# Stick-breaking scores from stacked key parts: two passes over doubled queries in place of three over a block diagonal

## The chip, the cores and the metric

The kernel runs on one core of one Trainium2 chip. The metric is the device time of one execution in microseconds: 546.92 us, the median of three runs (546.83 to 547.07). The engines are called PE (TensorE), DVE (VectorE), ACT (ScalarE), POOL (GpSimd) and SP (SyncE). PEld is PE's loading of the stationary operand, which overlaps the matmuls.

## The reference, cut to what matters

One layer of a decoder over 256 tokens of width 1024: a half-step feed-forward network, a mixer with two attentions side by side, a second half-step network, a final norm. All is float32. The change is in the second attention, stick-breaking, with 8 heads of 64:

```python
def stick_breaking_attention(q, k, v):
    z = einsum('bhqd,bhsd->bhqs', q, k) * scale          # scores, scale = 64 ** -0.5
    past = s_pos[None, :] < t[:, None]
    log_fail = where(past, log_sigmoid(-z), 0.0)
    later = cumsum(log_fail, axis=3, reverse=True) - log_fail
    w = where(past, exp(log_sigmoid(z) + later), 0.0)
    return einsum('bhqs,bhsd->bhqd', w, v)
```

A key's weight is its own sigmoid times the product of the failures of all keys between it and the query. A key later than the query has no weight, so of the 256 x 256 scores of a head the block of late keys (128 to 255) and early queries (0 to 127) isn't computed.

## The kernel before, in words

**Precision.** Each float32 operand is split into a high part in the matmul's format (fp32r) and the low rest, also fp32r. A product is three passes: high x high, high x low, low x high. `split` (L400) makes the two parts: a cast on ACT (L401), then a subtraction on DVE (L402). The weights stream in as tiles of 128 x 512 and are split the same way (L232 and L233 with a gain, L228 and L229 without), up to `AHEAD` = 7 tiles ahead of the matmul that uses them, in `WB` = 12 buffers.

**PE's order** is written out by hand. `unit` (L374) issues the three matmuls of 512 columns of one weight tile and one block of 128 tokens, then calls `weave.tick()` and `W.pump()`. So a tick, or step, is one unit of PE's stream. `Weave` (L102) holds generators that do the rest of the work: each runs to its next `yield d` and is due again d steps later. Those marked `long` (the two attention lanes) move one at a time per step, and after the others. `flush(long=True)` runs all of them to their ends without waiting for their steps.

**What sets the order of the others.** PE and SP follow the program's order. In this part of the kernel the instructions of ACT, DVE and POOL are put in order at compile time by a planner, from priorities and its own costs; on the chip each of these engines then takes its work strictly in that order.

**The mixer.** `project` (L876) makes one of ten projections of 512 columns: 8 weight tiles x 2 blocks of tokens = 16 units. In order: q, k, v of the MoBA attention (`heads(0, "a", ...)`), q, k, v of the stick-breaking one (`heads(3, "b", ...)`), four for the gates. Two lanes (L1080) run the attentions by pairs of heads between the units: pairs 0 and 2 in lane 0, pairs 1 and 3 in lane 1, MoBA first (`moba_pair`: scores S at L1006, then the softmax, the transposes `ptp` at L1024, the values `y_a` at L989), then stick-breaking (`stick_pair`). After the gates come the branch products `ba` and `bb`. After the first eight units of `ba` the lanes are flushed (L1141).

**q and k of the stick-breaking heads, turned.** A projection has tokens on the partitions; the scores need the head's 64 values there. DVE transposes 32 x 32 squares (L917) into `qsb` and `ksb`, and an exchange of 16 DMAs of 32 KB (`exchange`, L526), eight from SP and eight from POOL, moves the squares to their partitions in `qmb` and `kmb`. One step issues one DMA on each of the two queues. `D_LANDED` = 6 steps later the pieces are split, `D_PIECE` = 2 steps between them. k becomes `kThb` and `kTlb` (two casts of 128 x 512, two subtractions). q becomes a block diagonal, `bdhb` and `bdlb`, in two tiles each: with two heads on the 128 partitions, the columns of one head hold its queries on its 64 rows and zeros on the other 64 (eight memsets on POOL at L958, four casts and four subtractions of 64 x 512). `D_READY - D_PIECE` = 5 steps after the last piece, q or k is marked there, and `stick_pair` may start.

**The scores** (L1044 to L1047): one matmul with the block diagonal gives both heads, with 128 rows of contraction of which half meet zeros. `pass3` (L974) issues the three passes: 512 columns for the first 128 keys (2 heads x 256 queries), 256 columns for the last 128 keys (2 heads x 128 queries). Six matmuls and 2304 columns a pair, four pairs.

**Then**, at steps 7, 6, 6 and 6 apart (`D_STICK`): three activations on ACT, `sp` and its split on DVE with a mask on POOL between; the sums over later keys as matmuls with a triangle (L1064 to L1066); the exponential (L1068), mask and split to `wwh` and `wwl`; the product with the values (`values`, L989, `y_b`).

The tiles of 1024 columns named here (`big`, L281) share 20 buffers.

Of the kernel before, what the change touches and what calls it, by code (L numbers as in the profile page):

```python
# [8 lines left out]
F32 = mybir.dt.float32  # L9
# [8 lines left out]
P = 128  # L18
# [6 lines left out]
HD = 64  # L25
# [19 lines left out]
D_MOVE = 2  # L45
D_MOVED = 12
D_LANDED = 6
D_PIECE = 2
D_ROTATED = 14, 10
D_READY = 7  # L50
# [210 lines left out]
def hybrid_layer_kernel(ctx, tc, x, xt, pos, g_final, bgate, wstream, out):  # L261
    nc = tc.nc
# [18 lines left out]
    def big(nm, dt=F32R):  # L281
        return work.tile([P, 1024], dt, name=nm, tag="big", bufs=20)
# [12 lines left out]
    first = consts.tile([P, 3 * KD + T], F32, name="first")  # L295
# [45 lines left out]
    ident = consts.tile([P, P], F32, name="ident")  # L341
# [58 lines left out]
    def split(dst_h, dst_l, src, hi_engine=None, rest=nc.vector):  # L400
        (hi_engine or nc.scalar.copy)(dst_h, src)  # L401
        rest.tensor_sub(dst_l, src, dst_h.bitcast(F32))  # L402
# [105 lines left out]
    def lagged(n, lag):  # L508

        for k in range(n + lag):  # L510
            if k < n:
                yield 0, k
            if k >= lag:
                yield 1, k - lag

    def slots(q, n):

        return q[:, 0:n * P].rearrange("p (g s w) -> p s g w", g=4, s=n)

    def plain(q):
        return q.rearrange("p (s g w) -> p s g w", g=4, w=32)

    def exchange(moved, squares, n, queues, gap):  # L526

        w = 32
        for m in range(16):
            i, j = divmod(m, 4)  # L530
            queues[m % len(queues)].dma_start(moved[j * w:j * w + w, i * n * w:(i + 1) * n * w],  # L531
                                              squares[i * w:i * w + w, j * n * w:(j + 1) * n * w])
            if m % len(queues) == len(queues) - 1:
                yield gap
# [361 lines left out]
        g.tensor_mul(t2[:, :, 8:16], d3[:, :, 0:8], sin[:, t, 8:16].unsqueeze(1).to_broadcast([P, NH, 8]))  # L896
        marks["rot"] = g.tensor_add(d3[:, :, 0:16], t1, t2).ins

    def heads(b0, nm, res, rotary, diagonal):


        for j, which in enumerate("qk"):
            src = {}
            squares = None if rotary else big(f"{which}s{nm}", F32)

            def evac(t, ps, j=j, which=which, src=src, squares=squares):
                dst = row512(f"{which}{nm}{t}")
                if j == 0:
                    if nm == "a":
                        nc.gpsimd.tensor_scalar(rq[t], un[t].r, 0.125, None, op0=ALU.mult)  # L910
                    nc.scalar.activation(dst, ps, AF.Copy, scale=rq[t])
                else:
                    nc.scalar.activation(dst, ps, AF.Copy, scale=un[t].r)
                if rotary:
                    rotate(dst, t)
                else:
                    nc.vector.transpose(slots(squares, 8)[:, t:t + 7:2], plain(dst))  # L917
                src[t] = dst

            def turn(which=which, src=src, squares=squares):  # L920
                if rotary:
                    tp = two_banks(f"{which}tp{nm}")
                else:
                    tp = big(f"{which}m{nm}", F32)
                    yield from exchange(tp, squares, 8, [nc.sync, nc.gpsimd], 1)
                    yield D_LANDED
                for pr in range(4 if rotary else 0):
                    for t in range(2):
                        nc.tensor.transpose(tp[:, pr * 256 + t * P:pr * 256 + (t + 1) * P], src[t][:, pr * P:(pr + 1) * P], ident)
                if which != diagonal:  # L930
                    parts = big(f"{which}Th{nm}"), big(f"{which}Tl{nm}")
                    for c in range(2):
                        s = slice(c * 512, c * 512 + 512)
                        if rotary:
                            split(parts[0][:, s], parts[1][:, s], tp[:, s])
                        else:
                            split(plain(parts[0][:, s]), plain(parts[1][:, s]), slots(tp, 8)[:, c * 4:c * 4 + 4])
                            yield D_PIECE
                    ready = [[q[:, pr * 256:(pr + 1) * 256] for q in parts] for pr in range(4)]
                else:  # L940
                    tp4 = slots(tp, 8).rearrange("p (c t) g w -> p c t g w", t=2)
                    for c in range(2):
                        for j in range(2):
                            rows = slice(j * HD, j * HD + HD)
                            dst = [q[rows].rearrange("p (c j t g w) -> p c j t g w", c=2, j=2, t=2, g=4)[:, :, j] for q in res["bd"][c]]
                            split(dst[0], dst[1], tp4[rows, c * 2:c * 2 + 2])
                            yield D_PIECE
                    ready = [[q[:, pr % 2 * 512:pr % 2 * 512 + 512] for q in res["bd"][pr // 2]] for pr in range(4)]
                yield D_READY if rotary else D_READY - D_PIECE
                res[which] = ready  # L950

            if which == diagonal:
                res["bd"] = [(big(f"bdh{nm}{c}"), big(f"bdl{nm}{c}")) for c in range(2)]
                for c in range(2):
                    for q in res["bd"][c]:
                        for half in range(2):
                            q5 = q[half * HD:(half + 1) * HD].rearrange("p (c j t) -> p c j t", c=2, j=2)
                            nc.gpsimd.memset(q5[:, :, 1 - half, :].bitcast(F32), 0.0)  # L958
            project(b0 + j, evac)
            weave.add(turn(), D_ROTATED[j] if rotary else D_TURNED)  # L960

        vs = big(f"vh{nm}"), big(f"vl{nm}")

        def evac_v(t, ps):
            s = slice(t * 512, t * 512 + 512)
            nc.scalar.activation(vs[0][:, s], ps, AF.Copy, scale=un[t].r)
            nc.vector.scalar_tensor_tensor(vs[1][:, s], ps, un[t].r, vs[0][:, s].bitcast(F32),
                                           op0=ALU.mult, op1=ALU.subtract)
            if t == 1:
                res["v"] = [[q[:, s * 512:(s + 1) * 512] for q in vs] for s in range(2)]  # L970

        project(b0 + 2, evac_v)

    def pass3(o, a, b, first, last):  # L974
        for i, (p, q) in enumerate(((0, 0), (0, 1), (1, 0))):
            nc.tensor.matmul(o, a[p], b[q], start=first and i == 0, stop=last and i == 2, skip_group_check=True)

    def two(ap, w):
        return ap.rearrange("p (j w) -> p j w", w=w)
# [59 lines left out]
    def stick_pair(pr, b, y):  # L1039
        while "q" not in b or "k" not in b:  # L1040
            yield 0
        q, k = b["q"][pr], b["k"][pr]

        z = two_banks(f"z{pr}")  # L1044
        z0, z1 = two(z[:, 0:512], 256), two(z[:, 512:768], 128)
        pass3(z[:, 0:512], [e[:, 0:128] for e in k], q, True, False)
        pass3(z1, [e[:, 128:256] for e in k], [two(e, 256)[:, :, 128:256] for e in q], True, False)  # L1047
        zz = z[:, 0:768]
        e = wide(f"e{pr}")

        nc.scalar.activation(e, zz, AF.Abs)
        nc.scalar.activation(e, e, AF.Exp, scale=-1.0)
        nc.scalar.activation(e, e, AF.Ln, bias=1.0)
        b["z", pr] = True
        yield D_STICK[0]
        sp = wide(f"sp{pr}")
        nc.vector.scalar_tensor_tensor(sp, zz, 0.0, e, op0=ALU.max, op1=ALU.add)
        earlier(sp)
        sh, sl = wide_r(f"sh{pr}"), wide_r(f"sl{pr}")
        split(sh, sl, sp, nc.vector.tensor_copy)  # L1060
        yield D_STICK[1]
        for i, s in enumerate((sh, sl)):
            s1 = two(s[:, 512:768], 128)
            nc.tensor.matmul(z[:, 0:512], tri, s[:, 0:512], start=False, stop=False, skip_group_check=True)  # L1064
            nc.tensor.matmul(z1, tri, s1, start=False, stop=i == 1, skip_group_check=True)
            nc.tensor.matmul(z0[:, :, 128:256], ones, s1, start=False, stop=i == 1, skip_group_check=True)  # L1066
        w = wide(f"w{pr}")
        marks["exp"] = nc.scalar.activation(w, zz, AF.Exp).ins  # L1068
        earlier(w)
        yield D_STICK[2]  # L1070
        wh, wl = wide_r(f"wwh{pr}"), wide_r(f"wwl{pr}")
        split(wh, wl, w, nc.vector.tensor_copy)
        yield D_STICK[3]
        while "v" not in b:
            yield 0
        values(pr, b["v"], [two(e[:, 0:512], 256) for e in (wh, wl)], [two(e[:, 512:768], 128) for e in (wh, wl)], y, "b")

    a, b, ys = {}, {}, {}
# [22 lines left out]
    weave.add(lane(0), 36, long=True)  # L1101
    weave.add(lane(1), 42, long=True)
    heads(0, "a", a, True, None)
    heads(3, "b", b, False, "q")


    gates = {}
# [23 lines left out]
    for c in range(2):  # L1131
        banks = {}
        for t, k in lagged(4, 2):
            if k == 0:
                banks[t] = acc_bank(f"ba{t}{c}")
            i = W_BR + c * 4 + k
# [153 lines left out]
```

## Time and profile before

| | |
|---|---|
| median of three runs | 546.92 us (546.83 to 547.07) |
| profiled execution | 547.5 us |
| its span, first to last instruction | 545.8 us |
| PE busy | 538.0 us, 99% of the span, 2460 matmuls |
| weight loads (PEld) busy | 444.4 us, 2460 loads |
| DVE busy | 453.5 us, 83% |
| ACT busy | 355.5 us, 65% |
| POOL busy | 122.1 us, 22% |
| mean granted PE clock | 0.997 |

Times are microseconds; the duration of a single instruction in a group is in ns. A matmul's length in the trace holds the latency of the pipeline, so that neighbours overlap; what one costs is the distance from its start to the next one's. A group row gives line, engine, operation, output <- inputs, shapes, count, then busy time, mean ns of one, and the engine's idle time just before, with what ended it. A row for a tile has the least, median and greatest duration, and the first and last start. The chain of waits is the chain of work that ended last, with start and length of each piece.

### The profile page before, as it was taken

The page shows a single profiled execution, that of the slowest core. Times are in us where ns is not written, and L with a number is a line of the kernel's source. Part 1 is how long each engine was busy: PE and PEld are TensorE (multiplying, and loading weights), DVE is VectorE, ACT ScalarE, POOL GpSimd, SP SyncE. Part 2 cuts the span into 40 slices and gives each one's busy share as a digit, 9 for nine tenths or more (in the row PEclk, how much of TensorE's full clock was granted, in tenths as well). Part 3 has the DMA queues.
Part 4 walks back from the last instruction along what each step waited for, and adds up shares of the span by engine and source line. Part 5 has one row for each costly group of instructions (what it writes and reads, how often), then busy time and mean ns, then how long its engine had stood idle before and what let it go on. Part 6 is the DMA issues. An engine that isn't in the chain of part 4 may idle for free.

```text
span 545.8 us, 8032 instructions
## 1 busy us (share of the span) xinstructions
PE 538.0 (99%) x2460; PEld 444.4 (81%) x2460; DVE 453.5 (83%) x817; ACT 355.5 (65%) x620; POOL 122.1 (22%) x235
## 2 busy tenths in 40 slices
PE   9999999999999999999999999999999999999995
PEld 6888888888888888888888888888888888888884
DVE  5797799889999767889888888877667887899995
ACT  6776566667683777677875775466566566666843
POOL 2400000025503575022022200383000000265100
PEclk9999999999999999999999999999999999999998
DMA  8976765787866786455555354677657767787712
GB/s 280 406 263 220 239 209 184 231 254 225 257 225 191 274 261 217 154 155 191 170 161 175 125 188 153 195 244 233 215 180 223 221 201 236 233 227 237 238 49 77
DMA packets 44058, 114.84 MB, mean 210 GB/s; under 512 B 8512, under 2 KB 16240, under 8 KB 44016
## 3 DMA queue, kind: packets, MB, share of 16 engines
q1 hardware_dynamic: 37440, 106.68, 59.1%
q0 software_dynamic: 5904, 7.17, 6.0%
q10 hardware_dynamic: 672, 0.49, 0.3%
q8 instruction: 19, 0.31, 0.3%
q14 instruction: 23, 0.19, 0.1%
HBM read 104.87 MB, written 1.05 MB: 194 GB/s over the span
## 4 chain that ended last, share of the span: by engine, by line
PE 97%; DMA 1%; ACT 0%; SPq 0%; DVE 0%; issue 0%; ACTq 0%
PE gu_f L371 13%; PE gu_f L372 13%; PE gu_f L370 13%; PE in L370 7%; PE in L372 7%; PE in L371 7%; PE dn_f L371 5%; PE dn_f L372 5%; PE dn_f L370 5%; PE wo L372 1%; PE wo L370 1%; PE wo L371 1%; PE gu_f L383 1%; PE gu_f L384 1%; PE gu_f L386 1%; DMA raw<-in_wstream 1%
## 5 line engine op out<-in xcount | busy, mean ns | idle before, releaser
L233 DVE SCALAR_TENSOR_TENSOR wl<-raw,first,wh 128x512 fp32r<-128x512 f32 (+1 forms) x257 | 180.1, 742 | 24.0 <-ACT wh L232 23.5
L232 ACT ACTIVATE wh<-raw,first 128x512 fp32r<-128x512 f32 (+1 forms) x257 | 168.6, 714 | 26.1 <-PE gu_f L372 7.5
L229 DVE TENSOR_TENSOR wl<-raw,wh 128x512 fp32r<-128x512 f32 x120 | 78.7, 681 | 2.4 <-ACT wh L228 2.4
L228 ACT CAST wh<-raw 128x512 fp32r<-128x512 f32 x120 | 68.1, 618 | 18.2 <-PE bb L372 5.5
L371 PE MATMUL gu_f<-wl,zh 128*128 128x512 f32 x176 | 68.5, 389 | 0.0
L370 PE MATMUL gu_f<-wh,zh 128*128 128x512 f32 x176 | 68.5, 389 | 0.0
L372 PE MATMUL gu_f<-wh,zl 128*128 128x512 f32 x176 | 68.5, 389 | 0.0
L370 PE MATMUL in<-wh,uh 128*128 128x512 f32 x160 | 63.6, 397 | 0.0
L372 PE MATMUL in<-wh,ul 128*128 128x512 f32 x160 | 62.5, 391 | 0.0
L371 PE MATMUL in<-wl,uh 128*128 128x512 f32 x160 | 62.4, 390 | 0.0
L372 PE MATMUL gu_f<-wh,xl 128*128 128x512 f32 x144 | 56.0, 389 | 0.0
L370 PE MATMUL gu_f<-wh,xh 128*128 128x512 f32 x144 | 56.0, 389 | 0.0
L371 PE MATMUL gu_f<-wl,xh 128*128 128x512 f32 x144 | 56.0, 389 | 0.0
L200 POOL DMA_DIRECT2D raw<-in_wstream x10 | 9.4, 938 | 190.3 <-DVE cs_f L585 89.5
L370 PE MATMUL dn_f<-wh,hth_f 128*128 128x512 f32 x112 | 43.7, 390 | 0.0
L372 PE MATMUL dn_f<-wh,htl_f 128*128 128x512 f32 x112 | 43.6, 389 | 0.0
L371 PE MATMUL dn_f<-wl,hth_f 128*128 128x512 f32 x112 | 43.6, 389 | 0.0
L531 POOL DMA_DIRECT2D hm_f<-hs_f x64 | 34.3, 681 | 22.7 <-DMA raw<-in_wstream 9.3
L370 PEld LDWEIGHTS gu_f<-wh,zh 128*128 128x128 f32 x176 | 33.0, 188 | 6.9
L372 PEld LDWEIGHTS gu_f<-wh,zl 128*128 128x128 f32 x176 | 33.0, 188 | 6.8
L371 PEld LDWEIGHTS gu_f<-wl,zh 128*128 128x128 f32 x176 | 33.0, 188 | 6.8
L372 PEld LDWEIGHTS in<-wh,ul 128*128 128x128 f32 x160 | 30.0, 188 | 6.5
(320 smaller groups left out, 991.8 us busy)
## 6 DMA issues: line engine op xcount, KB each, us to landing
raw<-in_wstream SPq DMA_DIRECT2D x185, 512.0 KB, 4.5
hm_f<-hs_f SPq DMA_DIRECT2D x128, 32.0 KB, 4.1
raw<-in_wstream POOLq DMA_DIRECT2D x10, 256.0 KB, 4.6
raw<-in_wstream SPq DMA_DIRECT2D x5, 256.0 KB, 5.4
h<-in_x SPq DMA_DIRECT2D x2, 512.0 KB, 8.3
hm_f<-hs_f POOLq DMA_DIRECT2D x32, 32.0 KB, 3.9
bg<-in_bgate POOLq DMA_DIRECT2D x4, 256.0 KB, 5.1
xin<-in_xt SPq DMA_DIRECT2D x2, 256.0 KB, 6.6
```

The lines of the kernel that those rows point to most:

```text
L200: self.nc.gpsimd.dma_start(self.tile(s + 1), self.source(s), accum_op=ALU.add)
L228: self.nc.scalar.copy(hi, raw)
L229: self.nc.vector.tensor_sub(lo, raw, hi.bitcast(F32))
L232: self.nc.scalar.activation(hi[:, s], raw[:, s], AF.Copy, scale=g)
L233: self.nc.vector.scalar_tensor_tensor(lo[:, s], raw[:, s], g, hi[:, s].bitcast(F32), op0=ALU.mult, op1=ALU.subtract)
L370: nc.tensor.matmul(o, ah, wh, start=first, stop=False)
L371: nc.tensor.matmul(o, ah, wl, start=False, stop=False)
L372: nc.tensor.matmul(o, al, wh, start=False, stop=last)
L383: nc.tensor.matmul(o, ah, wh, start=first, stop=False)
L384: nc.tensor.matmul(o, al, wh, start=False, stop=False)
L386: nc.tensor.matmul(o, ah, wl, start=False, stop=last)
L531: queues[m % len(queues)].dma_start(moved[j * w:j * w + w, i * n * w:(i + 1) * n * w], squares[i * w:i * w + w, j * n * w:(j + 1) * n * w])
```

## The change

Keys and queries change places. The stationary operand becomes one tile per head with the key's high part on the upper 64 rows and its low part on the lower 64. The moving operand is the head's queries, written twice, on the upper and the lower rows. One pass over the queries' high part then gives high x high and low x high together, and a second over their low part high x low and low x low. Contraction is 128 rows without zeros. A head has its own matmuls: for each of the two heads and the two query parts 256 columns (first 128 keys) and 128 columns (last 128 keys), so eight matmuls and 1536 columns a pair.

To double the operands the exchange becomes `exchange_twice`: 32 DMAs of 32 KB instead of 16 for each of q and k, each square going to both halves of a tile of its head's parity (`moved[0]`, `moved[1]`). One step issues four, three on POOL and one on SP. The pieces come `D_LANDED_TWICE` = 9 steps after it. k: four casts of 128 x 512 and four subtractions, these on the lower 64 rows only and in place. q: four casts and four subtractions of 128 x 512. The block diagonal with its memsets, and `pass3`, go.

```diff
+D_LANDED_TWICE = 9
@@ in hybrid_layer_kernel
+    def exchange_twice(moved, squares, n, queues, gap):
+
+        w = 32
+        for m in range(32):
+            i, j, d = m // 8, m // 2 % 4, m % 2
+            row = d * HD + j % 2 * w
+            queues[m % len(queues)].dma_start(moved[j // 2][row:row + w, i * n * w:(i + 1) * n * w],
+                                              squares[i * w:i * w + w, j * n * w:(j + 1) * n * w])
+            if m % len(queues) == len(queues) - 1:
+                yield gap
@@ in heads
-                else:
-                    tp = big(f"{which}m{nm}", F32)
-                    yield from exchange(tp, squares, 8, [nc.sync, nc.gpsimd], 1)
-                    yield D_LANDED
...
-                            split(plain(parts[0][:, s]), plain(parts[1][:, s]), slots(tp, 8)[:, c * 4:c * 4 + 4])
-                            yield D_PIECE
                     ready = [[q[:, pr * 256:(pr + 1) * 256] for q in parts] for pr in range(4)]
                 else:
-                    tp4 = slots(tp, 8).rearrange("p (c t) g w -> p c t g w", t=2)
+                    moved = [big(f"{which}m{nm}{e}", F32) for e in range(2)]
+                    yield from exchange_twice(moved, squares, 8, [nc.gpsimd, nc.sync, nc.gpsimd, nc.gpsimd], 1)
+                    yield D_LANDED_TWICE
+                    parts = [[big(f"{which}{i}{nm}{e}") for i in range(1 if which == stacked else 2)] for e in range(2)]
+                    low = slice(HD, P) if which == stacked else slice(0, P)
                     for c in range(2):
-                        for j in range(2):
-                            rows = slice(j * HD, j * HD + HD)
-                            dst = [q[rows].rearrange("p (c j t g w) -> p c j t g w", c=2, j=2, t=2, g=4)[:, :, j] for q in res["bd"][c]]
-                            split(dst[0], dst[1], tp4[rows, c * 2:c * 2 + 2])
+                        s = slice(c * 512, c * 512 + 512)
+                        for e in range(2):
+                            hi, lo, raw = plain(parts[e][0][:, s]), plain(parts[e][-1][:, s]), slots(moved[e], 8)[:, c * 4:c * 4 + 4]
+                            nc.scalar.copy(hi, raw)
+                            nc.vector.tensor_sub(lo[low], raw[low], hi[low].bitcast(F32))
                             yield D_PIECE
-                    ready = [[q[:, pr % 2 * 512:pr % 2 * 512 + 512] for q in res["bd"][pr // 2]] for pr in range(4)]
+                    ready = [[[q[:, pr * 256:(pr + 1) * 256] for q in parts[e]] for e in range(2)] for pr in range(4)]
...
-            if which == diagonal:
-                res["bd"] = [(big(f"bdh{nm}{c}"), big(f"bdl{nm}{c}")) for c in range(2)]
-                for c in range(2):
-                    for q in res["bd"][c]:
-                        for half in range(2):
-                            q5 = q[half * HD:(half + 1) * HD].rearrange("p (c j t) -> p c j t", c=2, j=2)
-                            nc.gpsimd.memset(q5[:, :, 1 - half, :].bitcast(F32), 0.0)
@@ in stick_pair
-        pass3(z[:, 0:512], [e[:, 0:128] for e in k], q, True, False)
-        pass3(z1, [e[:, 128:256] for e in k], [two(e, 256)[:, :, 128:256] for e in q], True, False)
+        for first, outs in ((0, z0), (128, z1)):
+            for e in range(2):
+                for i, part in enumerate(q[e]):
+                    nc.tensor.matmul(outs[:, e], k[e][0][:, first:first + 128], part[:, first:256],
+                                     start=(e, i) == (0, 0), stop=False, skip_group_check=True)
@@ at the call
-    heads(3, "b", b, False, "q")
+    heads(3, "b", b, False, "k")
```

More of the change, by code (lines that the diff above doesn't have):

```diff
@@ L897, in rotate, with heads @@
         marks["rot"] = g.tensor_add(d3[:, :, 0:16], t1, t2).ins
-    def heads(b0, nm, res, rotary, diagonal):
+    def heads(b0, nm, res, rotary, stacked):
         for j, which in enumerate("qk"):
@@ L922, in turn @@
                     tp = two_banks(f"{which}tp{nm}")
-                else:
-                    tp = big(f"{which}m{nm}", F32)
-                    yield from exchange(tp, squares, 8, [nc.sync, nc.gpsimd], 1)
-                    yield D_LANDED
[L927 to L930, printed above, removed]
+                    for pr in range(4):
+                        for t in range(2):
+                            nc.tensor.transpose(tp[:, pr * 256 + t * P:pr * 256 + (t + 1) * P], src[t][:, pr * P:(pr + 1) * P], ident)
                     parts = big(f"{which}Th{nm}"), big(f"{which}Tl{nm}")
@@ L933, in turn @@
                         s = slice(c * 512, c * 512 + 512)
-                        if rotary:
-                            split(parts[0][:, s], parts[1][:, s], tp[:, s])
-                        else:
-                            split(plain(parts[0][:, s]), plain(parts[1][:, s]), slots(tp, 8)[:, c * 4:c * 4 + 4])
-                            yield D_PIECE
+                        split(parts[0][:, s], parts[1][:, s], tp[:, s])
                     ready = [[q[:, pr * 256:(pr + 1) * 256] for q in parts] for pr in range(4)]
@@ L972, in heads @@
         project(b0 + 2, evac_v)
-    def pass3(o, a, b, first, last):
-        for i, (p, q) in enumerate(((0, 0), (0, 1), (1, 0))):
-            nc.tensor.matmul(o, a[p], b[q], start=first and i == 0, stop=last and i == 2, skip_group_check=True)
     def two(ap, w):
```

## The prediction

> **What bounds the kernel now.** I read the page first, then the PE instructions around the scores, then who writes and reads the tiles of the exchange.
>
> ```profile
> span 545.8 us, 8032 instructions
> PE 538.0 (99%) x2460; PEld 444.4 (81%) x2460; DVE 453.5 (83%) x817; ACT 355.5 (65%) x620; POOL 122.1 (22%) x235
> PE 97%; DMA 1%; ACT 0%; SPq 0%; DVE 0%; issue 0%; ACTq 0%
> ```
>
> PE sets the end: 97% of the chain that ended last is matmuls. So a microsecond taken off PE's stream is a microsecond off the span, and work on another engine costs only where PE then waits. There are as many weight loads as matmuls (2460 each): each matmul has its own load, also where the weights repeat.
>
> The profiled execution took 547.5 us (span 545.8 and 1.7 around it), 0.58 us above the median of the runs, 546.92. I make the sum against 547.5 and take 0.58 off at the end.
>
> **The scores on PE.** The first pair, in order of time (start us, length with the pipeline's latency), and the same six instructions in the chain of waits:
>
> ```profile
> 268.74 0.39 PE L976 MATMUL z<-bdhb,kTlb 128*128 128x512 f32 x1
> 268.96 0.28 PE L976 MATMUL z<-bdhb,kThb 128*128 128x256 f32 x1
> 269.08 0.28 PE L976 MATMUL z<-bdlb,kThb 128*128 128x256 f32 x1
> 269.20 0.28 PE L976 MATMUL z<-bdhb,kTlb 128*128 128x256 f32 x1
> 269.32 0.40 PE L370 MATMUL in<-wh,uh 128*128 128x512 f32 x1
> 268.45 1.03 PE z L976 x6
> ```
>
> What counts is from start to start: 0.12 us for 256 columns. Three of 512 and three of 256 take 1.03, so 512 columns take (1.03 - 0.36) / 3 = 0.223. The change has four matmuls of 256 columns (two heads, two parts of the queries) and four of 128 for each pair: 1536 columns for 2304, but eight loads for six. The first four cost 4 x 0.12 = 0.48. A 128-column matmul over 128 rows with such operands is not in the trace; the nearest rows are the MoBA scores, whose two heads run side by side on 64 rows each, and the transposes:
>
> ```profile
> 249.29 0.23 PE L1006 MATMUL S<-kTha,qTha 64*128 64x128 f32 x2
> 249.29 0.19 PEld L1006 LDWEIGHTS S<-kTla,qTha 64*128 64x128 f32 x2
> 249.35 0.28 PE L1006 MATMUL S<-kTla,qTha 64*128 64x128 f32 x2
> 249.40 0.19 PEld L1006 LDWEIGHTS S<-kTha,qTla 64*128 64x128 f32 x2
> 249.46 0.27 PE L1006 MATMUL S<-kTha,qTla 64*128 64x128 f32 x2
> 227.64 0.66 PE ptp L1024 x6
> ```
>
> Both heads' loads start together, so this is one load per row group, and the next follows 0.11 us later (249.29, 249.40); the last two pairs of 128-column matmuls are also 0.11 apart, though their columns alone are half those of a 0.12 matmul. The transposes, 128 rows by 128 columns, take 0.66 / 6 = 0.11 each. So I read 0.11 us as the price of one load that has no longer matmul to hide behind. Bounds for the 128-column matmul: below, the line through 512 and 256 columns, 0.12 - (0.223 - 0.12) / 2 = 0.0685, if loads hid altogether; above, 0.12, as if it were as long as the 256. I take 0.11, since that row is nearest (same column count, a load each). A pair then costs 0.48 + 4 x 0.11 = 0.92 for 1.03, **0.11 saved, 0.44 for four pairs**; bounds 0.28 x 4 = 1.1 and 0.07 x 4 = 0.28.
>
> The Trainium skill has a rule that speaks against this change ("TensorE: Matmul & The Clock Gate", section "LDWEIGHTS (loading the stationary operand)"): a load takes P / 1.2 ns for P columns, whatever the rows, so 107 ns for 128 columns. The trace's 0.11 agrees, and by the rule the sum would be 0.48 + 4 x 0.107 = 0.91, the same. The same page, section "Back-to-back issue gap", gives 81 ns for a load and a matmul of 128 columns in a stream; by that the saving would be about 0.9 us, and no row here shows it.
>
> **The exchange, pieces and buffers.** Who writes and reads the exchanged tiles now, and the cleared diagonals:
>
> ```profile
> L531 POOL DMA_DIRECT2D qmb<-qsb x8: 496/497/601, 234.6 to 238.1; - x8
> L401 ACT CAST bdhb<-qmb x4: 608/616/622, 241.9 to 248.1; 64x512 fp32r<-64x512 f32 x4
> L402 DVE TENSOR_TENSOR bdlb<-qmb,bdhb x4: 642/680/690, 243.0 to 250.7; 64x512 fp32r<-64x512 f32 x4
> DMA to landing us min/median/max: 1.7/3.5/4.1
> L531 POOL DMA_DIRECT2D kmb<-ksb x8: 496/496/498, 248.9 to 252.3; - x8
> L401 ACT CAST kThb<-kmb x2: 605/612/618, 261.6 to 262.1; 128x512 fp32r<-128x512 f32 x2
> L402 DVE TENSOR_TENSOR kTlb<-kmb,kThb x2: 681/682/683, 262.7 to 263.3; 128x512 fp32r<-128x512 f32 x2
> L958 POOL MEMSET bdhb<- 64x512 f32 x4 | 2.1, 528 | 0.1
> L531 POOL DMA_DIRECT2D qmb<-qsb x8 | 4.0, 510 | 19.7 <-PE in L372 19.7
> ```
>
> *POOL and SP.* SP issues 8 DMAs for each of q and k, as before. POOL goes from 8 to 24 for each: at 0.497 us, 11.9 us for q (234.6 to 246.5) and, begun at 248.9, to 260.8 for k. Eight memsets go (two groups like the quoted one, 4.2 us), but POOL then sat idle 19.7 us, so nothing is gained. The last q transfer lands 3.5 us after its issue, at 250.0, the last of k near 264.3; the first piece of q needs 21 of POOL's 24, at 248.5.
>
> *ACT and DVE.* q keeps four casts and four subtractions, k goes from two of each to four: ACT 2 x 0.61 = 1.2 us, DVE 2 x 0.68 = 1.4 us more. What hides it is the lead of the weights, whose splits fill both engines:
>
> ```profile
> core 0: us, PE busy (x) PEld busy (x) DVE busy (x) ACT busy (x) POOL busy (x), PEclk, DMA share, GB/s
> 249.00:256.00 7.00, 7.00 (x41) 5.81 (x42) 6.86 (x12) 4.36 (x10) 3.83 (x8) 1.00 0.55 158
> 256.00:263.00 7.00, 7.00 (x36) 5.83 (x35) 6.41 (x15) 6.39 (x17) 0.00 (x0) 1.00 0.59 201
> 263.00:269.00 6.00, 6.00 (x30) 5.00 (x29) 5.57 (x10) 4.14 (x9) 0.00 (x0) 1.00 0.49 175
> 253.76 0.75 DVE L233 SCALAR_TENSOR_TENSOR wl<-raw,first,wh 128x512 fp32r<-128x512 f32 x1
> 263.14 0.39 PE L370 MATMUL in<-wh,uh 128*128 128x512 f32 x1
> ```
>
> DVE is 98% busy from 249 to 256. The last two rows are the 52nd of the 80 projection tiles, finished at 254.51 and first used at 263.14: 8.6 us, the shortest lead of all eighty. A delay of 1.4 us is taken from that; cost nothing. Without the lead it would be 1.4.
>
> *Steps.* One step is one `unit`, three matmuls, about 0.685 us. Counted from the end of the q projection, k's exchange starts at step 19. Before: eight issue steps, then 6, two pieces of 2, then 5: k is there at 42. After: 9 for 6, and four pieces for two: 3 + 4 = 7 later, at 49. The first scores start at 268.29 now, so seven steps on, 273.1; k's last piece lands at 264.3 and needs 4 x 0.61 and a subtraction, so it is done by 269 with some 4 us over. All four pairs slide by seven steps, and nothing on PE waits for that until the lanes are flushed, at step 104 (a rival below).
>
> *Buffers.* q's four parts are drawn at step 20 instead of the diagonals before the projection; by my count of the 20 `big` tiles they must reuse those of the MoBA queries and keys, whose last reader is the MoBA score of pair 3 (to 249.66, just past the rows above). So no q piece runs before about 249.7, when its transfers have landed anyway.
>
> **The sum**: 547.5 - 0.44 = 547.06 on the profiled execution's scale, 0.58 less for the median: **546.5 us**, 0.08% less.
>
> **Rivals.**
>
> *1. The loads hide* (faster). If 128-column matmuls ran at 0.0685 us, 1.1 us are saved: **545.8**. For it: the second pair of matmuls above follows the first by only 0.06. Against: the loads themselves keep 0.11, and so do the transposes.
>
> *2. Late landing stops ACT* (slower). Here is the place:
>
> ```profile
>   ACT uh L401: 3.0, 2
> 258.50 0.27 DVE L1020 TENSOR_SCALAR p<-p,st 128x128 f32<-128x128 f32 x1
> 259.06 0.82 PE L1024 MATMUL ptp<-ident,p 128*128 128x128 f32 x6
> ```
>
> The last MoBA pair's probabilities are ready at 258.77 and PE transposes them from 259.06: 0.3 us of slack, far less than the weights have. ACT takes its work in order. The old first q cast ran at 241.9; three steps later is 244.0, and if the planner put the new one there, ACT would stand until 248.5 or, held by the buffer, 249.7, with DVE's subtraction behind it, and the pair's exponentials queue behind both. That is up to 5 us, of which ACT's idle time from 249 to 256 (7 - 4.36 = 2.6) gives back half: PE waits some 2.3, **548.8**. For it: the first row, from the exchange ahead of the projections, where ACT did wait 3.0 us in all for transfers. Against: there PE lost nothing by it, in the q exchange itself ACT shows no wait now, and the pair's own work (step 19) stands ahead of the pieces (20) in the program. It decides from 1.5 + 0.3 = 1.8 us of delay, where the 0.44 saved and the 1.1 of the bound are used up.
>
> *3. The flush catches the last pair.* The last pair now, from its sums over later keys (L1064) to its product with the values:
>
> ```profile
> 310.27 0.39 PE L1064 MATMUL z<-sh,sums 128*128 128x512 f32 x1
> 314.62 0.96 DVE L402 TENSOR_TENSOR wwl<-w,wwh 128x768 fp32r<-128x768 f32 x1
> 320.48 0.51 PE L989 MATMUL y_b<-wwh,vhb 128*128 128x512 f32 x2
> 321.53 0.40 PE L370 MATMUL ba<-wh,yah 128*128 128x512 f32 x1
> ```
>
> Its weights are ready 5.3 us after the sums start (315.58 - 310.27) and used after 10.2, at step 102. Seven steps later that would be 109, but the flush at 104 sends it at once. Between lie the sums themselves (about 0.94), seven units (4.8) and pair 2's product (1.05): 6.8 us against 5.3, so 1.5 to spare. Its chain passes ACT, POOL and DVE; if each found 0.7 us of other work ahead, PE would wait 0.6: **547.1**.
>
> **Chances and range.** The forecast 0.52, rival 1 0.13, rival 2 0.20, rival 3 0.10, something else 0.05. About 0.2% (1.1 us) is what a measurement of this kernel can tell from no change. Rival 1 ends on that line, so half of it counts as faster, with the forecast's own lucky tail 0.15. Slower is rival 2 for the most part, with the tails of 3 and the unknown order of ACT and DVE: 0.22. The rest, 0.63, is no difference. The range goes from rival 1 with a little over, 545.6, to rival 2's price, 548.9; the forecast's own is 545.9 to 547.2.
>
> **What would show it.** Eight z matmuls per pair that take 0.92 in the chain of waits, the 128-column ones 0.11 apart (0.07 for rival 1); the first z seven units later than now; POOL issuing 24 DMAs back to back from 234.6 and 248.9; no idle time of PE before L1024 at the last MoBA pair (rival 2) nor before the last y_b, which should come two units later than now, after the eighth ba unit (rival 3). ACT waiting on the exchanged tiles without PE waiting would leave the forecast whole. I am wrong if PE's stream between 185 and 340 us is longer than now, or if the 128-column matmuls are priced otherwise.

## The result, and the profile after

The changed kernel takes 550.03 us (median of six executions, 549.40 to 551.67) beside 547.00 for the kernel before (546.51 to 548.12) on the same chip: a ratio of **1.0056, 95% interval 1.0039 to 1.0072**. It is slower by some 3 us, above the upper end of the range of the prediction (548.9). The profiled execution took 551.67 us, the longest of the six; the kernel before took 547.5 in its own.

The page of the changed kernel, its first lines (line numbers of the changed kernel are one higher than before up to the exchange; behind it the difference varies):

```profile
span 550.0 us, 8111 instructions
PE 539.9 (98%) x2468; PEld 444.0 (81%) x2468; DVE 454.7 (83%) x819; ACT 356.0 (65%) x622; POOL 133.8 (24%) x259
```

PE has eight matmuls more, POOL 24 instructions more (32 transfers for eight memsets), DVE and ACT two each, as the diff says. The span grew by 4.2 us and PE's busy time, whose ends are modelled, by 1.9: PE stands longer than before.

**Where it went.** Both kernels issue the same 714 units of PE in the same order, so the start of each can be subtracted from its start before. The jumps of that difference between units, in the changed kernel's profiled execution, and in a second profile of the same kernel (the run after_again below), worked out from the rows of PE's timeline. For the scores it is the net of a pair, four times; at the last y_b it is the jump less the 1.05 us of the product itself:

```
stretch, us                               profiled   again
the first unit                              -0.33    -0.84
188 to 190   u ahead of the projections     +1.45    +0.16
259 to 268   last MoBA pair                 +1.04    +0.53
275 to 308   the four pairs' scores         -0.46    -0.46
about 324    last y_b                       +1.11    +1.13
379 to 383   z of the second network        +1.21    +1.83
the last unit                               +4.06    +2.39
```

The small rest is drift. The second line is all but gone in the second profile: ACT's cast of u, whose exchange the change doesn't touch, waits 3.6 us for transfers in the first and 2.65 in the second, and I count the difference as chance. The other four are the result.

*The scores.* One pair on PE (start us, length with the pipeline's latency):

```profile
275.21 0.28 PE L1046 MATMUL z<-q0b,k0b 128*128 128x256 f32 x1
...
275.56 0.28 PE L1046 MATMUL z<-q1b,k0b 128*128 128x256 f32 x1
275.68 0.22 PE L1046 MATMUL z<-q0b,k0b 128*128 128x128 f32 x1
275.74 0.28 PE L1046 MATMUL z<-q1b,k0b 128*128 128x128 f32 x1
275.86 0.27 PE L1046 MATMUL z<-q0b,k0b 128*128 128x128 f32 x1
275.97 0.27 PE L1046 MATMUL z<-q1b,k0b 128*128 128x128 f32 x1
276.08 0.44 PE L371 MATMUL in<-wh,uh 128*128 128x512 f32 x1
276.36 0.39 PE L372 MATMUL in<-wl,uh 128*128 128x512 f32 x1
```

and, in the kernel before, the second matmul behind its pair (the pair starts at 268.29):

```profile
269.55 0.40 PE L371 MATMUL in<-wl,uh 128*128 128x512 f32 x1
```

From start to start of the pair alone, 276.08 - 275.21 = 0.87 for 1.03 before. But the first 512-column matmul behind the pair is now followed after 0.28 (276.08 to 276.36), before after 0.23 (269.32 to 269.55): a part of the price falls on it. With it a pair takes 276.36 - 275.21 = 1.15 for 269.55 - 268.29 = 1.26. So **0.11 are saved a pair**; the trace's ns give 0.114, 0.46 for four.

*The last MoBA pair.* The q exchange, ACT and the transposes:

```profile
235.40 8.97 POOL L523 DMA_DIRECT2D qmb<-qsb  x18 [23.92 <-DVE qsb L929]
245.09 0.50 POOL L523 DMA_DIRECT2D qmb<-qsb  x1 [0.71 <-DMA qmb<-qsb]
...
248.05 1.47 POOL L523 DMA_DIRECT2D qmb<-qsb  x3 [0.81 <-DMA qmb<-qsb]
250.75 1.14 ACT L953 CAST q0b<-qmb 128x512 fp32r<-128x512 f32 x2 [1.65 <-DMA qmb<-qsb]
252.20 0.42 DVE L403 TENSOR_TENSOR yal<-y_a,yah 64x256 fp32r<-64x256 f32 x1 [1.14 <-ACT yah L402]
260.36 1.06 PE L1021 MATMUL ptp<-ident,p 128*128 128x128 f32 x6
260.55 0.27 DVE L1017 TENSOR_SCALAR p<-p,st 128x128 f32<-128x128 f32 x1
```

The brackets give the idle time of the engine before the instruction and what ended it. POOL issues 18 transfers without a gap, then stands four more times (0.71, 0.18, 0.49 and 0.81 us) and ends at 249.5. Each time it goes on 0.28 us after the transfer eight places ahead of the next one has landed: the 19th of q starts at 245.09, and the 11th landed at 244.81. The 21st, the last that the first cast needs, lands at 250.29; the cast stands on ACT until 250.75, 1.65 us, and DVE stands 1.14 us behind it. The last pair's probabilities are ready at 260.82, two microseconds later than before, and the transposes, 0.82 long before, are stretched to 1.06: they begin while the last columns are still being scaled. The stretch costs 0.42 there and 0.6 in the three places behind it.

*The last y_b.* ACT, DVE and PE after the flush:

```profile
320.08 2.01 ACT L1145 ACTIVATE gate<-gate 128x1024 f32<-128x1024 f32 x2
321.74 0.94 DVE L403 TENSOR_TENSOR wwl<-w,wwh 128x768 fp32r<-128x768 f32 x1
322.00 0.35 ACT L402 CAST ybh<-y_b 64x256 fp32r<-64x256 f32 x1
322.25 1.06 ACT L1145 ACTIVATE gate<-gate 128x1024 f32<-128x1024 f32 x1
323.65 0.37 ACT L402 CAST ybh<-y_b 64x256 fp32r<-64x256 f32 x1 [0.34 <-DVE ybl L403]
324.05 0.43 DVE L403 TENSOR_TENSOR ybl<-y_b,ybh 64x256 fp32r<-64x256 f32 x1 [0.43 <-ACT ybh L402]
324.62 0.58 PE L986 MATMUL y_b<-wwh,vhb 128*128 128x512 f32 x2 [0.89 <-DVE ybl L403]
```

The weights of pair 3 are there at 322.68. What PE waits for is the bank: `y_bank` has one buffer, pair 2's product lies in it, and its two halves are read out by a cast and a subtraction each. On ACT the first cast stands behind two of the gates' sigmoids (L1145) that the program starts at the flush, the second behind one more. In the kernel before, the last subtraction of pair 2 was well ahead of pair 3's product (at 320.48):

```profile
318.45 0.43 DVE L402 TENSOR_TENSOR ybl<-y_b,ybh 64x256 fp32r<-64x256 f32 x1
```

*z of the second network.* POOL's part of an exchange that the change doesn't touch, in the kernel before:

```profile
365.95 2.04 POOL L531 DMA_DIRECT2D zm<-zs  x4 [0.67 <-issue]
ACT zh L401 <- DMA zm<-zs: 0.6, 1, 0.6
```

and after:

```profile
368.79 0.56 POOL L543 DMA_DIRECT2D zm<-zs  x1 [0.67 <-DVE zs L468]
372.17 1.48 POOL L543 DMA_DIRECT2D zm<-zs  x3 [2.81 <-issue]
```

What ACT and PE of the changed kernel waited for (us in all, times, longest), as in the second line above for the kernel before:

```profile
ACT zh L402 <- DMA zm<-zs: 4.6, 1, 4.6
PE y_b L986 <- DVE ybl L403: 0.9, 1, 0.9
PE gu_f L371 <- ACT zh L402: 0.6, 1, 0.6
```

Between the first and the second transfer POOL stands 2.81 us on nothing that the profile names. ACT, which waited 0.6 us for zm before, waits 4.6, and PE waits behind it, at `gu_f`. In the kernel before the same kind of stop stands elsewhere, in the last exchange but one, where nobody waits for it:

```profile
499.06 2.45 POOL L531 DMA_DIRECT2D hm_f<-hs_f  x5 [2.36 <-issue]
```

Counted from the start of the kernel, both are POOL's 129th transfer. It isn't the wait for the transfer eight places ahead: in the changed kernel that one had landed at 360.79, 11 us earlier. The theory which the experiments test is that the stop goes with the count: the change has put 32 transfers ahead, and so moved it from an exchange with time to spare into one without.

### The profile page after: what moved, and what is told of

Read it like the earlier page. It is cut to its first block, busy times and chain, and to the rows that moved or that the text cites. A ratio compares the mean times of both kernels' runs of the same rounds, so it can differ in the third digit from the quotient of the medians.

```text
span 550.0 us, 8111 instructions
## 1 busy us (share of the span) xinstructions
PE 539.9 (98%) x2468; PEld 444.0 (81%) x2468; DVE 454.7 (83%) x819; ACT 356.0 (65%) x622; POOL 133.8 (24%) x259
## 3 DMA queue, kind: packets, MB, share of 16 engines
HBM read 104.87 MB, written 1.05 MB: 193 GB/s over the span
## 5 line engine op out<-in xcount | busy, mean ns | idle before, releaser
L371 PEld LDWEIGHTS in<-wh,uh 128*128 128x128 f32 x160 | 30.1, 188 | 7.7 <-ACT uh L402 1.3
```

Source lines behind the costliest of these rows:

```text
L371: nc.tensor.matmul(o, ah, wh, start=first, stop=False)
```

## The experiments

The kernels ran beside the kernel before on the same chip; each ratio is to it, with its 95% interval.

**1. The changed kernel again.**

> The changed kernel itself once more, to tell waits that return from waits that one profiled execution happened to have. In its first profile four places hold PE longer than before: 1.4 us before the projections (188 to 190, ACT waits for the u exchange, which the change doesn't touch), 1.1 us from 259 to 268 (the last MoBA pair, behind ACT's wait for the q exchange), 1.1 us at the last y_b (322 to 325.7), 1.2 us in the second network's first products (379 to 381, ACT waits 4.6 us for the zm exchange). If the first is chance it is gone here, and the other three, which add to 3.4 and less the 0.5 saved on the scores make 2.9, return; time 549.5 to 550.5. If the zm wait is chance too, it is gone and the profiled span is nearer to 547.5.

550.01 us, 1.0051 (1.0039 to 1.0063). The delay at 188 to 190 is all but gone; the shorter scores and the three stalls are there, each stall with the same wait. So they belong to the change.

**2. The scores alone.** The kernel before with the new shape of the scores; the block diagonal, its memsets and the old exchange stay. The keys' low part isn't multiplied.

```diff
-        pass3(z[:, 0:512], [e[:, 0:128] for e in k], q, True, False)
-        pass3(z1, [e[:, 128:256] for e in k], [two(e, 256)[:, :, 128:256] for e in q], True, False)
+        for first, outs in ((0, z0), (128, z1)):
+            for e in range(2):
+                for i, part in enumerate(q):
+                    nc.tensor.matmul(outs[:, e], k[0][:, first:first + 128], part[:, e * 256 + first:e * 256 + 256],
+                                     start=(e, i) == (0, 0), stop=False, skip_group_check=True)
```

> The kernel before with only the scores' shape on PE changed: eight matmuls per pair (four of 256, four of 128 columns), same exchange, same steps. It leaves out the pass of the keys' low part, so the values are of lower precision. If a 128-column matmul costs its load (0.11 us), a pair takes 0.92 for 1.03 and the time is 0.44 us less than before: ratio 0.9992. If the loads hide, 1.1 us less: 0.998. Nothing waits, since no step moves.

546.61 us beside 547.22, 0.9988 (0.9980 to 0.9997): 0.6 us less, with the forecast's 0.44 well inside the interval (0.2 to 1.1). In its trace PE gains 0.43 between 267 and 400 and waits for nothing from 180 to 400. The first part of the change is worth what its matmuls cost, and all the rest, 3.4 us (550.01 - 546.61), is the price of the exchange and of the steps.

**3. Nothing but the transfers.** The kernel before, with 32 transfers of 32 KB on POOL at a time when it is idle, into tiles that nobody reads:

```diff
+                for n in range(2):
+                    pad = big(f"pad{n}", F32)
+                    for m in range(16):
+                        nc.gpsimd.dma_start(pad[m // 4 * 32:m // 4 * 32 + 32, m % 4 * 256:m % 4 * 256 + 256],
+                                            h[0][m // 4 * 32:m // 4 * 32 + 32, m % 4 * 256:m % 4 * 256 + 256])
                 res["bd"] = [(big(f"bdh{nm}{c}"), big(f"bdl{nm}{c}")) for c in range(2)]
```

> The kernel before with 32 DMAs of 32 KB more on POOL, put where POOL is idle (before the q exchange, from about 215 us), into tiles nobody reads; scores and steps as before. Theory of a POOL queue that stops at a fixed count: in the kernel before POOL stood still 2.4 us at about its 129th DMA, in the second network's turn exchange, where nobody waits; in the changed kernel, with 32 more, it stood 2.8 us at about the same count, which is now the second DMA of the zm exchange, and PE lost 1.2 us there. Then this kernel, too, shows a wait of POOL of 2 to 3 us in zm, ACT waiting for zm 4 us or more, and about 1.2 us more time: 548.2, ratio 1.002. Rival, chance or contention in that place: POOL goes through zm as in the kernel before (0.7 us) and the time stays within 0.3 us of before.

549.62 us, 1.0048 (1.0030 to 1.0066), more than expected. The stop is at the second zm transfer again:

```profile
365.72 0.56 POOL L531 DMA_DIRECT2D zm<-zs  x1 [0.67 <-ACT zh L401]
369.11 1.48 POOL L531 DMA_DIRECT2D zm<-zs  x3 [2.82 <-issue]
```

PE loses 1.4 us there. Nothing of the change is in this kernel but the number of transfers, so the number alone brings the stall. What the trace shows is not the whole of the median, though: its profiled execution is the lowest of its seven (548.67), and another 0.7 us that it lost lie at about 254, at a y_a product. The padding cost something of its own.

**4. The lanes four steps earlier.** The changed kernel, with no wait behind the last piece, so that keys and queries are marked ready at step 45:

```diff
-                yield D_READY if rotary else D_READY - D_PIECE
+                yield D_READY if rotary else 0
```

> The changed kernel with the stick-breaking q and k marked there 4 steps sooner after their last piece (1 step for 5), so that the first scores come at step 45 for 49. Theory for the last y_b: it is sent by the flush four steps after pair 2's, into the one PSUM bank that pair 2's result still holds, whose evacuation stands behind the sigmoids on ACT; with pair 2's at step 96 and the last again eight steps behind, its wait (0.9 us) and the slower start after it are gone: 1.1 us less than the changed kernel, about 548.9. Rival, that the weights wwl are what is late: the same gain, but the profile of the changed kernel has them ready at 322.7, 1.9 us before the matmul. If instead the first scores now wait for k's last piece (done about 270.7), PE waits at z and up to 1 us is lost again.

548.85 us, 1.0025 (1.0014 to 1.0035): 1.2 us back. PE's wait for `ybl` is gone, the delays at the last MoBA pair (0.9) and at zm (1.5) are still there. The flush's stall came from the slide of the lanes.

**5. The stop on another transfer.** The changed kernel with two more transfers on POOL ahead of the q projection of the stick-breaking heads, so that the 129th is the load of the final gain `gB`:

```diff
+        if not rotary:
+            pad = big("pad", F32)
+            for m in range(2):
+                nc.gpsimd.dma_start(pad[0:32, m * 256:m * 256 + 256], h[0][0:32, m * 256:m * 256 + 256])
```

> The changed kernel with two more 32 KB DMAs on POOL before the q exchange, so that the 129th DMA of POOL's queue is the load of the final gain, for which nobody waits till the end, and no longer the second DMA of the zm exchange. Theory of the count: POOL stands 2.8 us at that load, the zm exchange runs through, ACT waits under 1.5 us for zm and PE's 1.2 to 1.8 us before the second network's products (379 to 382) are gone: 1.2 to 1.8 us less than the changed kernel, 548.3 to 548.8. Rival, that the longer POOL queue or the changed order of ACT delays zm: two DMAs more change nothing, 550.0.

549.64 us, 1.0044 (1.0032 to 1.0056): a miss, most of the gain didn't come. POOL stood at the right place, and for zm it was the wrong one:

```profile
355.51 3.92 POOL L543 DMA_DIRECT2D zq<-zq  x8 [1.29 <-DVE zq L449]
362.03 0.55 POOL L1197 DMA_DIRECT2D gB<-in_g_final  x1 [2.59 <-PE wo L373]
...
368.40 2.05 POOL L543 DMA_DIRECT2D zm<-zs  x4
```

The load stands from 359.44 to 362.03. The releaser in the bracket is inferred and doesn't settle it: PE signals at the end of each unit, every 0.68 us, and in the profiles of before and after the same load follows the transfer ahead of it with no gap. POOL then works through its part of the norm of z and reaches the first zm transfer 12.9 us after the second group of zq (355.51 to 368.40), where the changed kernel took 11.4 (357.39 to 368.79). PE still loses 0.8 at zm, and ACT still waits 4.2 for it. A stop that isn't in the exchange but on POOL's way to it costs there too.

**6. q's pieces five steps later.** The other cure for ACT's wait for q: 14 steps behind the exchange.

```diff
-                    yield D_LANDED_TWICE
+                    yield D_LANDED_TWICE + (5 if which == "q" else 0)
```

> The changed kernel with the pieces of q five steps later (14 steps behind the exchange for 9), k's unchanged at 9. Theory: ACT stood 1.7 us at the first piece of q, whose transfers had not landed, and the last MoBA pair's softmax behind it made PE wait in small pieces, 0.5 to 1.1 us in all from 259 to 268. Five steps are 3.4 us, so ACT should no longer wait for qmb, and PE loses nothing before the transposes and the values of that pair: 0.5 to 1 us less than the changed kernel, 549.0 to 549.5, with the waits at the last y_b and at zm left. Rival, that DVE is simply full there (86 to 98% busy) and the pieces cost what they cost wherever they lie: no gain, or the stall moves to the v projection's evacuation or to k's pieces.

550.36 us, 1.0060 (1.0045 to 1.0074): no gain. The stall moves to k's pieces, as the last words of the rival had it. ACT waits less for q and all the more for k, and now another product stands behind it:

```profile
248.71 0.62 ACT L953 CAST q0b<-qmb 128x512 fp32r<-128x512 f32 x1 [0.60 <-DMA qmb<-qsb]
...
263.17 0.62 ACT L953 CAST k0b<-kmb 128x512 fp32r<-128x512 f32 x1 [3.08 <-DMA kmb<-ksb]
263.70 0.72 ACT L233 ACTIVATE wh<-raw,first 128x512 fp32r<-128x512 f32 x1
264.32 0.78 ACT L402 CAST ph<-ptp 128x768 fp32r<-128x768 f32 x1
```

PE's wait there:

```profile
PE y_a L986 <- ACT ph L402: 1.0, 1, 1.0
```

The step count fixes only when the program offers a piece; where the planner then sets it in ACT's order is another matter. Why it set k's first piece ahead of its transfers here, the trace doesn't say.

**7. Half of the exchange on each queue.** The changed kernel with 16 transfers on POOL and 16 on SP:

```diff
-[nc.gpsimd, nc.sync, nc.gpsimd, nc.gpsimd]
+[nc.gpsimd, nc.sync, nc.gpsimd, nc.sync]
```

> The changed kernel with the 32 DMAs of each exchange half on SP, half on POOL (POOL 16 for 24, SP 16 for 8), steps unchanged. POOL has 16 DMAs less in all, so its 129th falls into the second network's turn exchange as in the kernel before: no wait in zm, 1.2 to 1.8 us back. POOL's last q transfer is issued 4 us sooner, so ACT should not wait for qmb: 0.5 to 1 us back. The wait at the last y_b, 1.1 us, stays. Together 547.5 to 548.3. Against it: SP issues 8 DMAs of 0.58 us more among the weight loads, and q's last transfers on SP may now be the late ones; then only the zm part comes back, 548.5.

548.22 us, 1.0017 (1.0007 to 1.0027): 1.8 us back. The delay at the last MoBA pair and that at zm are both gone, y_b keeps its 1.1. The 129th transfer is now in the exchange of hm_f again, where nobody waits:

```profile
487.18 3.95 POOL L543 DMA_DIRECT2D hm_f<-hs_f  x8 [2.45 <-issue]
```

**8. Both.** Half on each queue, and the lanes four steps earlier (edits 7 and 4).

> Both together: exchanges half on SP, half on POOL, and q and k marked there four steps sooner. All three waits gone, what is left is the shorter scores (0.16 us a pair in the two profiles, 0.64 us): 546.5 to 546.9, which would be faster than the kernel before (547.2 in these runs). If a wait stays at the last MoBA pair, 547.0 to 547.5.

546.67 us beside 547.07, 0.9994 (0.9985 to 1.0003). PE has no wait left between 180 and 400. The whole change is in it; it is 3.4 us under the changed kernel's 550.03 and can't be told from the kernel before. In its profile PE gains 0.43 us between 267 and 400, as with the scores alone (and loses 0.5 behind 510, which no other profile here shows and whose cause is open). POOL's issue of q is short, and ACT's casts no longer wait:

```profile
233.40 7.48 POOL L523 DMA_DIRECT2D qmb<-qsb  x15 [23.93 <-DVE qsb L929]
241.39 0.50 POOL L523 DMA_DIRECT2D qmb<-qsb  x1 [0.51 <-DMA qmb<-qsb]
```

The tile's row (ns min, median, max; first and last start):

```profile
L953 ACT CAST q0b<-qmb x4: 614/636/658, 247.0 to 250.3; 128x512 fp32r<-128x512 f32 x4
```

**9. and 10. The stop where POOL is idle.** Experiments 5 and 7 left it open whether the count is the cause: 5 kept most of the delay, and 7 changed the exchange too. So, the changed kernel with 22 more transfers (32 rows of 64 columns each) between the k exchange and that of z, and the same with edit 4:

```diff
+    pad = work.tile([P, 512], F32, name="pad", tag="bg", bufs=2)
+    with tc.issue_after(marks["rot"]):
+        for m in range(22):
+            nc.gpsimd.dma_start(pad[m // 8 * 32:m // 8 * 32 + 32, m % 8 * 64:m % 8 * 64 + 64],
+                                h[0][m // 8 * 32:m // 8 * 32 + 32, m % 8 * 64:m % 8 * 64 + 64])
     merged = {(t, c): row512(f"m{t}{c}") for t in range(2) for c in range(2)}
```

> Done: the changed kernel with 22 more transfers issued by POOL after the gates' biases, at about 290 us, where POOL is idle till 312; each copies 32 rows of 64 columns to a tile that nobody reads, so nothing of the computation is left out. POOL's 129th transfer is then one of these instead of the second zm transfer. Theory (the zm stall is the stop of POOL's queue at its 129th transfer, put there by the 32 extra transfers of the change): the 2.8 us stand at about 300 us on POOL with no one waiting, the zm transfers follow each other, ACT waits under 1 us for zm, and PE's delay there (1.2 to 1.8 us) is gone: 548.2 to 548.8, with 0.6 us less for the scores and 1.1 us at the last y_b as in the changed kernel. Rival (the stall is of the zm exchange itself, whatever POOL issued before): POOL stands at zm as before and the time stays at 550.0.

> Done: the same 22 transfers, and the last wait of the pieces 0 steps instead of 4, so that keys and queries are called ready at step 45 instead of 49. Theory: the stall at zm and the one at the last y_b are both gone, and what remains of the change is the delay between 255 and 270 us (0.5 to 1.1) less 0.6 for the scores: 547.0 to 547.8, that is the kernel before within 0.15%, with the exchange still at 24 transfers on POOL. Rival (the two stalls cover each other or others): only one of the two gains is seen, 548.3 to 549.0.

The first took 549.37 us, 1.0035 (1.0021 to 1.0049), over what was expected; the second 547.95, 1.0011 (1.0002 to 1.0019), within it. In the first, the stop is on the 129th transfer, now a padding one, and zm goes through:

```profile
313.02 1.73 POOL L1126 DMA_DIRECT2D pad<-h  x3
316.08 0.98 POOL L1126 DMA_DIRECT2D pad<-h  x2 [1.33 <-issue]
317.07 1.28 POOL L1033 TENSOR_SCALAR_AFFINE_SELECT w<-w 128x256 f32<-128x256 f32 x2
...
367.61 2.04 POOL L543 DMA_DIRECT2D zm<-zs  x4 [0.67 <-DVE zs L468]
```

Its waits of ACT and PE:

```profile
ACT zh L402 <- DMA zm<-zs: 0.4, 1, 0.4
PE y_b L986 <- DVE ybl L403: 1.6, 1, 1.6
```

PE loses nothing at zm, so the rival, a stall of the zm exchange itself, falls. But the padding began at 301.8 and not at 290: it ran into the lanes' masks on POOL (L1033), DVE's work behind them came later, and the wait at the last y_b grew from 0.9 to 1.6 us. These 0.7 us are about what the first missed by. With the lanes four steps earlier that wait is gone as well, and what stays is the last MoBA pair (1.2).

**The account.** By the medians: from the changed kernel to experiment 4, 1.2 us for the flush; from there to 10, 0.9 for zm; from 10 to 8, 1.3 for the q and k exchange on POOL: 3.3 in all, each with its wait in the trace. Not all of these ran side by side, and each step is uncertain by about 0.1%, 0.5 us; that each wait goes with its edit is seen in the traces, its exact share of the time is not.

## Why the prediction was wrong

The forecast was 546.5 us, 0.44 less than before, and gave 0.63 to no difference. Its one term, the scores, was right, and three waits that it had set at nothing or left out took 3.4 us in the first profile and 3.5 in the second.

**The scores: right.** Forecast 0.92 us a pair and 0.11 saved; measured 0.87 for the eight matmuls and 0.05 on the 512-column one behind them, 0.92 in all, and 0.114 saved. The first 128-column matmul is followed after 0.06 (275.68 to 275.74), the other three after 0.11 to 0.12. Who counts the pair alone reads 0.16 saved and 0.64 for four; the unit behind it takes a third of that back. Rival 1, whose loads hide, falls. By the rule that the prediction took from the Trainium skill ("TensorE: Matmul & The Clock Gate", section "LDWEIGHTS (loading the stationary operand)"), 107 ns for each load of 128 columns, a pair was to take 0.91, and the trace agrees; the 81 ns of "Back-to-back issue gap" are not reached, with 0.11 for each of the four once the matmul behind them is counted.

**"POOL ... 11.9 us" for q: the step that failed first.** I multiplied 24 by 0.497 and had them follow each other. The row that I read it from had eight transfers, too few for POOL to wait on its own earlier ones. POOL's transfers take turns on eight semaphores (the counters that tell of a landing), and in none of the twelve profiles does one start less than 0.28 us after the landing of the one eight places ahead. Eight issues take 3.9 us, so nothing is seen of it while a transfer lands within 3.6. The median was like before, but the 11th to 18th took 4.4 to 5.8 us (min, median and max over all of q, for 1.7/3.5/4.1 before):

```profile
DMA to landing us min/median/max: 1.7/3.6/5.8
```

Why these landed late, no run shows. So POOL stood 0.71, 0.18, 0.49 and 0.81 us and ended at 249.5 in place of 246.5 (with a start 0.8 later). The 21st landed at 250.29, where I had 248.5. The profile of before had the same wait, in an exchange with 16 transfers on POOL, a row that the prediction doesn't use:

```profile
491.35 0.99 POOL L531 DMA_DIRECT2D hm_f<-hs_f  x2 [0.61 <-DMA hm_f<-hs_f]
```

The buffers, which were to hold the pieces until 249.7, did not hold the casts: in experiment 8 two of them ran from 247.0, ahead of the last MoBA score of pair 3 (248.57).

**"Cost nothing" for ACT and DVE, and rival 2.** For the weights this held: PE never waited for a `wh` or `wl` there. For the MoBA pair it didn't, and rival 2, which named the pair, the transposes and 0.3 us of slack, was the mechanism. Its size was over: 2.3 us forecast, 0.5 to 1.0 in the two profiles. The planner had the first cast behind the `ph` cast on ACT, so that ACT stood 1.65 us and not the "up to 5" that I took (its own times, 244.0 to 248.5 or 249.7, give 4.5 to 5.7). The chance of 0.20 was too low, for the reason in the step above. Its point, that 1.8 us of delay decide, fell: 1.65 cost 1.04, more than twice what the scores gave.

**Rival 3: the place was right, the resource was not.** I measured the flush by `wwl`, found 1.5 us to spare, and gave it 0.10. `wwl` did come in time, 1.9 us ahead of its use (322.68 and 324.62). But pair 3's product also needs the bank of pair 2's, and between these two I had only counted their 1.05 us on PE. Before, they were far enough apart for the evacuation (the last `ybl` of pair 2 starts at 318.45, pair 3's product at 320.48); after, the flush sends the second four units behind the first, with two sigmoids, 2.01 us, in front of the first cast and one of 1.06 in front of the second. It cost 1.1, where the rival had 0.6. Experiment 4 takes it away with the slide alone.

**Left out: the zm exchange.** My working on POOL's 24 transfers ended with the k exchange. Nothing of it looked at what stands behind them on POOL's queue 100 us later. The stop at the 129th transfer was in the trace of before, 2.36 us idle with no releaser, in a place without a waiter. That 32 more transfers would move it 32 places forward, into the second network's first exchange, could have been read only by someone who had tied it to the count. Experiments 3, 7, 9 and 10 show it.

**What held.** The eight memsets gone gave nothing. The first z came seven units later, and the last y_b two units later than before, as counted. POOL's DMAs began at once (235.4). The forecast's sentence on what would prove it wrong named a longer stream of PE between 185 and 340 us; the stream is longer there, and then again behind it.

## What to carry to other kernels

An exchange on a queue isn't priced by its issues alone: ask how many transfers the queue has out before it waits for its own (eight here), how long they take to land, and what else on that queue is moved, to the end of the kernel. Where a flush or a slide brings two products closer together, look at the buffer that they share, and at what its evacuation queues behind, before the operands of the second. Measure a shortened group of matmuls up to the second one behind it, since the next may pay a part. And a saving of 0.46 us on the bounding engine needs every other engine's order to stay where it was: here three small delays, none of them on PE's own work, cost seven times that.

## What the hardware did that was not expected

**POOL's queue stands up to 2.8 us at its 129th transfer.** It did so in each kernel here, wherever that transfer fell: 2.36 us in hm_f before, 2.81 in zm after, 2.82 in the kernel before with 32 more transfers, 2.45 in hm_f with half of the exchange on SP, 2.59 at gB. Among the small padding transfers it was shorter, 1.33 and 1.12. Transfers of 256 KB, 32 KB and 8 KB count alike. It is the first of the 17th turn of the eight semaphores; why it is that number stays open, and no kernel here reaches a 257th.

**POOL never has more than eight of its transfers out.** In all twelve profiles each starts at least 0.28 us after the landing of the one eight places ahead, and at just 0.28 where that was the wait: 0.2 to 1.6 us at a time for the 32 KB transfers of q, k and the padding. In the kernel before the q exchange, with eight on POOL, shows none; the hm_f exchange, with 16, shows 0.16, 0.22 and 0.61. Whether the eight is the chip's or the program's as built, no run here shows.

**The matmul behind a group of short ones pays a part of their price.** Four of 128 columns behind four of 256 are 0.06, 0.12, 0.11 and 0.11 us apart, 0.40 in all; the 512-column matmul behind them takes 0.28 for 0.23.
